# Strassen weight sums for gate and up: from VectorE subtractions to accumulating DMA transfers

## The chip, the core and the metric

The kernel runs on one core of a Trainium2 chip. Its engines work side by side, each with a queue of its own that it takes in order: TensorE (PE) multiplies matrices, VectorE (DVE) and ScalarE (ACT) do elementwise work, GpSimd (POOL) does little here, SyncE (SP) only issues DMA transfers. ACT and POOL can issue transfers as well. All of them run on the same 16 DMA engines. The metric is the device time of one execution in microseconds; lower is better.

## The reference

One decoder layer on 512 tokens of width 2048, in float32: a norm, four token mixers side by side, an output projection, and then the part that matters here, the feed-forward network:

```
def swiglu(h, w_gate, w_up, w_down):
    return (jax.nn.silu(h @ w_gate) * (h @ w_up)) @ w_down
...
        h = rmsnorm(x, norm_ffn_g[l])
        x = x + swiglu(h, w_gate[l], w_up[l], w_down[l])
```

`w_gate` and `w_up` are 2048 x 5632, `w_down` is 5632 x 2048.

## The kernel before

The stages follow one another: input projection and mixers, output projection (whose last pass also makes the sums of x for the next stage), gate and up, down, final norm.

*Exact products from rounded ones.* A float32 operand is split in two: ACT copies it into a rounded high half, DVE subtracts that from the operand to get the low half (`split2`, L1045; its two instructions carry the lines L1047 and L1048). Each product is three matmuls, high by high, high by low, low by high (L1297 to L1299).

*Strassen.* Gate and up are computed in 11 weight groups of 512 columns. In each group the tokens (two halves), the inputs (two halves, kh) and gate against up (f) form 2 x 2 blocks, and Strassen's scheme in Winograd's form takes seven block products in place of eight, in the order P1, P5, P6, P3, P7, P4, P2. P1, P3 and P2 take a weight block as it is, the other four take sums of weight blocks. A product is four steps of 12 matmuls (two input blocks of 128 rows, two token blocks, three matmuls each), so a group has 28 steps and the stage 308. Which sums of x a product takes is prepared once, in `first_sums` and `last_sums`, with their halves in `cmb`.

*Weights.* `w_dma` (L1113) issues the loads on SP, 256 KB each, into tiles wq, at most 12 at a time; blocks that two products need are loaded again (FRESH has five entries, so ten loads for each quarter of a group). `w_sum` (L1125) makes the sums on DVE: T = B12 - B11 for P5, B22 - T for P6, B21 - T for P4, in place in a tile T of 512 KB, and B22 - B12 for P7 (L1131, L1135, L1139, L1143). `w_split` (L1145) makes the two halves. High halves have 3 buffers, low halves 4.

*Order.* The program order is written out. Ahead of step k, `w_ahead` (L1157) makes sums for steps up to k+3 and splits for steps up to k+2, and issues loads for steps up to k+7:

```
        w_dma(k + 4)
        while sw["add"] < min(k + 4, len(steps)):
            ...
            w_sum(sw["add"])
            sw["add"] += 1
            if sw["split"] < min(k + 3, sw["add"]):
                w_split(sw["split"])
```

Results are read out of PSUM in `got_product` (L1253), by ACT (L1257, L1271) or by a DVE addition (L1266, L1268, L1275). `turn_h` (L1177) is side work spread over the following steps: it applies the norm and the gate, transposes h on PE, forms the sums of h for the down stage and stores them in DRAM from ACT's queue (hs, sh, sl, hT; ten stores of 256 KB a group). For the first group, the last sums of x (`late_sums`) run beside the first steps. POOL issues no transfer anywhere.

Of the kernel before, what the change touches and what calls it, by code (L numbers as in the profile page):

```python
# [8 lines left out]
F32 = mybir.dt.float32  # L9
F32R = mybir.dt.float32r  # L10
AF = mybir.ActivationFunctionType
OP = mybir.AluOpType
# [27 lines left out]
def hybrid_kernel(ctx, tc, xT, wi, wt, wo, wgu, wdn, vec, rows, sgw, w2a2, g2, pbias, cmask, oneh, addc, fing, out):  # L40
    nc = tc.nc
    pe, dv, ac, gp = nc.tensor, nc.vector, nc.scalar, nc.gpsimd
# [12 lines left out]
    def t2(name, shape=(128, 512), dt=F32):  # L55
        return p2.tile(list(shape), dt, name=name, tag="s2")
# [130 lines left out]
    for j in range(KT):  # L187
        t = t2("xraw")
# [829 lines left out]
    fp = sums.enter_context(tc.tile_pool(name="fp", bufs=4, reuse_waits="tile"))  # L1018
# [5 lines left out]
    norm2 = RowNorm()  # L1024
# [20 lines left out]
    def split2(hi, src, lo):  # L1045

        ac.activation(hi, src, AF.Copy)  # L1047
        dv.tensor_sub(lo, src, hi.bitcast(F32))  # L1048
# [8 lines left out]
    def first_sums(j):  # L1057

        a, b = xg[j], xg[j + 8]
        s12 = s2[j] = t2("s12")  # L1060
        dv.tensor_add(s12[:, lo_t], a[:, hi_t], b[:, hi_t])
        dv.tensor_sub(s12[:, hi_t], s12[:, lo_t], a[:, lo_t])
        h12, l12 = t2("h12", dt=F32R), t2("l12", dt=F32R)
        split2(h12, s12, l12)
        cmb["P5", j] = h12[:, lo_t], l12[:, lo_t]
        cmb["P6", j] = h12[:, hi_t], l12[:, hi_t]

        dv.tensor_sub(s12[:, lo_t], b[:, lo_t], s12[:, hi_t])

    def last_sums(j):  # L1070

# [22 lines left out]
    def ffn_norm():  # L1094
        while len(sqs) > 1:
            add_squares()
            yield
        for _ in range(8):
            yield
        norm2.add(sqs.pop(0))  # L1100
        norm2.root()
        yield


    ORDER = ("P1", "P5", "P6", "P3", "P7", "P4", "P2")
    FRESH = dict(P1=(0, 0), P5=(0, 1), P6=(1, 1), P7=(0, 1), P4=(1, 0))
    NGR = NG // 4
    steps = [(gi, p, jj) for gi in range(NGR) for p in ORDER for jj in range(4)]
    sw = dict(dma=0, add=0, split=0)
    raw, T, src, cut = {}, {}, {}, {}  # L1110
    RAWS = 12

    def w_dma(limit):  # L1113
        while sw["dma"] < min(limit, len(steps)):
            gi, p, jj = steps[sw["dma"]]
            if p in FRESH:
                if len(raw) + 2 > RAWS:
                    return
                kh, f = FRESH[p]
                for j in (2 * jj, 2 * jj + 1):  # L1120
                    t = raw[kh, f, j] = t2("wq")
                    nc.sync.dma_start(t, wgu[gi, kh, f, j])
            sw["dma"] += 1

    def w_sum(k):  # L1125
        gi, p, jj = steps[k]
        js = (2 * jj, 2 * jj + 1)
        if p == "P5":
            T[jj] = fp.tile([128, 2, 512], F32, name="T")
            for u, j in enumerate(js):  # L1130
                dv.tensor_sub(T[jj][:, u], raw.pop((0, 1, j)), raw.pop((0, 0, j)))  # L1131
            src[k] = T[jj]
        elif p == "P6":
            for u, j in enumerate(js):
                dv.tensor_sub(T[jj][:, u], raw[1, 1, j], T[jj][:, u])  # L1135
            src[k] = T[jj]
        elif p == "P4":
            for u, j in enumerate(js):
                dv.tensor_sub(T[jj][:, u], raw[1, 0, j], T[jj][:, u])  # L1139
            src[k] = T.pop(jj)  # L1140
        elif p == "P7":
            for j in js:
                dv.tensor_sub(raw[1, 1, j], raw[1, 1, j], raw.pop((0, 1, j)))  # L1143

    def w_split(k):  # L1145
        gi, p, jj = steps[k]
        hi = wp.tile([128, 2, 512], F32R, name="wh", tag="wraw", bufs=3)
        lo = wp.tile([128, 2, 512], F32R, name="wl", tag="wsp", bufs=4)
        if p in ("P5", "P6", "P4"):
            split2(hi, src.pop(k), lo)  # L1150
        else:
            for u, j in enumerate((2 * jj, 2 * jj + 1)):
                q = {"P1": (0, 0), "P3": (1, 1), "P7": (1, 1), "P2": (1, 0)}[p] + (j,)
                split2(hi[:, u], raw.pop(q) if p in ("P7", "P2") else raw[q], lo[:, u])
        cut[k] = hi, lo

    def w_ahead(k):  # L1157

        w_dma(k + 4)
        while sw["add"] < min(k + 4, len(steps)):  # L1160
            if sw["add"] >= sw["dma"]:
                w_dma(sw["add"] + 1)
            w_sum(sw["add"])
            sw["add"] += 1
            if sw["split"] < min(k + 3, sw["add"]):
                w_split(sw["split"])
                sw["split"] += 1
        while sw["split"] < min(k + 3, len(steps)):
            w_split(sw["split"])
            sw["split"] += 1  # L1170
        w_dma(k + 8)

    part = {}
# [3 lines left out]
    def turn_h(gi, th, h, us):  # L1177

        def put(p, t, u=0):
            nc.scalar.dma_start(ad[PI[p] + u, gi], t.rearrange("p (b t) -> p b t", b=2))  # L1180

        def high(p, src):
            hi = t2("sh", dt=F32R)
            ac.activation(hi, src, AF.Copy)
            put(p, hi.bitcast(F32))
            return hi

        def low(src, hi):
# [12 lines left out]
        if th == 0:  # L1201
            yield
            for t in range(2):
                ac.activation(h[t], h[t], AF.Silu, scale=rn[t])
        yield
        for t in range(2):
            dv.scalar_tensor_tensor(h[t], us[t], rn[t], h[t], op0=OP.mult, op1=OP.mult)
        us.clear()
        yield
        yield  # L1210
        p = turned(0)
        a = t2("hT")
# [36 lines left out]
        lo = low(p, hi)  # L1249
        yield  # L1250
        put("P2", lo.bitcast(F32), 1)
# [57 lines left out]
    for g in range(8):  # L1309
        def on_last(b, acc, g=g):  # L1310
            make_x2(g + 8 * b, acc)
            if b:
                split_a11(g)
                if g:
                    first_sums(g - 1)
                square_x2(g)
                square_x2(g + 8)
                if g:
                    add_squares()
                if g == 4:  # L1320
                    w_dma(4)
                if g == 6:
                    for j in range(3):
                        last_sums(j)
            elif g == 7:
                for j in range(3, 5):
                    last_sums(j)

        def early(g=g):
            if st["split"] < len(chunks):  # L1330
                issue_split()
            else:
                w_split(sw["split"])
                sw["add"] = sw["split"] = sw["split"] + 1
        brs = (2, 0)[g < 5:]
        run(gemm(len(brs), lambda c, k: (yh[brs[c], k], yl[brs[c], k]), on_last, early))
    for br in (0, 2):
# [306 lines left out]
def _layout(inp):  # L1644
# [15 lines left out]
    wt = np.ascontiguousarray(w.reshape(8, 2, 128, 4, 512).transpose(3, 0, 2, 1, 4))  # L1660
    wo = f("w_out")[0].reshape(2048, 2, 8, 128).transpose(0, 2, 1, 3)
    wo = np.ascontiguousarray(wo.reshape(4, 4, 128, 8, 256).transpose(3, 0, 2, 1, 4))
    gu = np.stack([f("w_gate")[0].reshape(2, 8, 128, 11, 512), f("w_up")[0].reshape(2, 8, 128, 11, 512)])
    wgu = np.ascontiguousarray(gu.transpose(4, 1, 0, 2, 3, 5))
    wdn = f("w_down")[0].reshape(11, 2, 2, 128, 2, 1024).transpose(0, 2, 1, 4, 3, 5)
    wdn = np.ascontiguousarray(wdn).reshape(22, 2, 2, 128, 1024)
    fing = f("norm_final_g").reshape(2, 1024)
# [31 lines left out]
```

## Time and profile before

| | |
|---|---|
| median of 3 runs | 2318.23 us (2317.65 to 2318.55) |
| profiled execution | 2319.38 us, span 2317.6 us |
| PE busy | 2231.3 us, 96% |
| DVE busy | 1562.3 us, 67% |
| ACT busy | 1014.6 us, 44% |
| POOL busy | 2.3 us, 16 instructions |
| gate and up stage | about 932 to 1836 us of the span |

A line is the line of the kernel's source; a helper's line stands for all its callers. A name such as wl<-wq,wh gives the tile written and those read. Busy time of PE is modelled, since matmuls are pipelined: the pace shows in the distance between their starts. Idle time is put down to what released the engine.

### The profile page before, as it was taken

The numbers are of one execution on the slowest core, as the hardware profiler recorded it, in microseconds if no ns is written. First come the engines' busy times: TensorE is split into PE (matmuls) and PEld (weight loads), VectorE is DVE, ScalarE is ACT, GpSimd is POOL, SyncE is SP. The second block draws the span as 40 slices with busy tenths as digits, with TensorE's granted clock in tenths as the row PEclk, the third lists the DMA queues.
The fourth block names the chain that finished last, engine by engine and source line by source line (L and its number), as shares of the span: only waits on it lengthen the run. The fifth ranks groups of instructions, "written<-read, shape, count | busy, mean of one in ns | idle before, by whom it ended". The sixth has DMA issues, their size and how long they took to land.

```text
span 2317.6 us, 29310 instructions
## 1 busy us (share of the span) xinstructions
PE 2231.3 (96%) x11064; PEld 1787.2 (77%) x11064; DVE 1562.3 (67%) x2345; ACT 1014.6 (44%) x1552; POOL 2.3 (0%) x16
## 2 busy tenths in 40 slices
PE   8999999999999998799999999999999799999996
PEld 6788878877777776587778778777877678888884
DVE  6555456654444456887877877887787677777765
ACT  5522231234445444544544454455445344543334
POOL 0000000000000000000000000000000000000000
PEclk9999999999999999899999999999999999999998
DMA  5222323222223334344653555465355277438884
GB/s 187 82 92 82 104 67 94 71 91 76 79 73 118 100 114 142 113 167 146 196 170 118 176 164 167 146 200 168 118 173 195 93 286 249 162 118 271 290 302 154
DMA packets 164542, 342.79 MB, mean 148 GB/s; under 512 B 29296, under 2 KB 34928, under 8 KB 164400
## 3 DMA queue, kind: packets, MB, share of 16 engines
q1 hardware_dynamic: 135408, 291.30, 38.9%
q10 hardware_dynamic: 28992, 49.61, 6.1%
q8 instruction: 87, 1.43, 0.3%
q14 instruction: 55, 0.45, 0.1%
HBM read 302.79 MB, written 38.05 MB: 147 GB/s over the span
## 4 chain that ended last, share of the span: by engine, by line
PE 82%; DVE 9%; ACT 4%; DMA 2%; issue 2%; ACTq 0%; SPq 0%; DVEq 0%
PE prod L1298 10%; PE prod L1299 10%; PE prod L1297 10%; PE acc L145 7%; PE acc L147 7%; PE acc L146 7%; PE bk L1383 5%; PE bk L1384 5%; PE bk L1382 5%; PE acc L166 3%; PE acc L168 3%; PE acc L167 3%; DVE wl L1048 2%; DMA wq<-in_wgu_dram 1%; ACT wh L1047 1%
## 5 line engine op out<-in xcount | busy, mean ns | idle before, releaser
L1048 DVE TENSOR_TENSOR wl<-wq,wh 128x512 fp32r<-128x512 f32 x352 | 227.0, 686 | 138.6 <-ACT wh L1047 137.5
L1298 PE MATMUL prod<-wl,h 128*128 128x512 f32 x704 | 276.8, 393 | 17.4 <-DVE wl L1048 17.4
L1047 ACT ACTIVATE wh<-wq 128x512 fp32r<-128x512 f32 x352 | 202.5, 623 | 186.7 <-PE prod L1299 112.1
L1297 PE MATMUL prod<-wh,h 128*128 128x512 f32 x704 | 276.4, 393 | 0.0
L1299 PE MATMUL prod<-wh,l 128*128 128x512 f32 x704 | 274.2, 390 | 0.0
L1382 PE MATMUL bk<-dh,ah 128*128 128x512 f32 x608 | 239.7, 394 | 25.5 <-ACT dh L1047 25.5
L107 DVE TENSOR_TENSOR wlo<-wraw,whi 128x1024 fp32r<-128x1024 f32 x127 | 155.3, 1223 | 148.0 <-ACT whi L106 147.7
L1383 PE MATMUL bk<-dl,ah 128*128 128x512 f32 x608 | 239.7, 394 | 3.2 <-DVE dl L1048 3.2
L1384 PE MATMUL bk<-dh,al 128*128 128x512 f32 x608 | 238.4, 392 | 0.0
L106 ACT ACTIVATE whi<-wraw 128x1024 fp32r<-128x1024 f32 x127 | 133.9, 1054 | 196.9 <-PE acc L146 94.3
L145 PE MATMUL acc<-xhi,whi 128*128 128x512 f32 x512 | 209.3, 409 | 5.3 <-ACT whi L121 5.2
L1047 ACT ACTIVATE wh<-T 128x1024 fp32r<-128x1024 f32 x132 | 140.2, 1062 | 153.2 <-PE prod L1299 83.5
L147 PE MATMUL acc<-xhi,wlo 128*128 128x512 f32 x512 | 201.0, 393 | 1.1 <-DVE wlo L107 1.1
L146 PE MATMUL acc<-xlo,whi 128*128 128x512 f32 x512 | 201.0, 393 | 0.3 <-DVE xlo L239 0.3
L1048 DVE TENSOR_TENSOR wl<-T,wh 128x1024 fp32r<-128x1024 f32 x132 | 161.0, 1220 | 36.2 <-ACT wh L1047 35.4
L1298 PEld LDWEIGHTS prod<-wl,h 128*128 128x128 f32 x704 | 132.2, 188 | 53.0 <-DVE wl L1048 26.6
L1297 PEld LDWEIGHTS prod<-wh,h 128*128 128x128 f32 x704 | 132.2, 188 | 29.9 <-ACT wh L1047 3.1
L1382 PEld LDWEIGHTS bk<-dh,ah 128*128 128x128 f32 x608 | 115.4, 190 | 50.9 <-ACT dh L1047 27.1
L1299 PEld LDWEIGHTS prod<-wh,l 128*128 128x128 f32 x704 | 132.2, 188 | 27.1
L1047 ACT ACTIVATE dh<-T 128x1024 fp32r<-128x1024 f32 x66 | 70.0, 1060 | 171.8 <-DVE T L1461 55.6
L1297 PE MATMUL prod<-wh,hb 128*128 128x512 f32 x352 | 140.1, 398 | 4.8 <-DVE c L1268 4.8
L1383 PEld LDWEIGHTS bk<-dl,ah 128*128 128x128 f32 x608 | 115.3, 190 | 30.5 <-DVE dl L1048 6.8
(316 smaller groups left out, 4155.9 us busy)
## 6 DMA issues: line engine op xcount, KB each, us to landing
wq<-in_wgu_dram SPq DMA_DIRECT2D x440, 256.0 KB, 3.5
rw<-in_wdn_dram SPq DMA_DIRECT2D x134, 512.0 KB, 4.9
wraw<-in_wi_dram SPq DMA_DIRECT2D x63, 512.0 KB, 3.6
wraw<-in_wt_dram SPq DMA_DIRECT2D x32, 512.0 KB, 3.6
wraw<-in_wo_dram SPq DMA_DIRECT2D x32, 512.0 KB, 3.7
ar<-ad SPq DMA_DIRECT2D x44, 256.0 KB, 3.9
ad<-sh ACTq DMA_DIRECT2D x33, 256.0 KB, 3.7
ad<-hs ACTq DMA_DIRECT2D x33, 256.0 KB, 4.1
```

Source lines behind the costliest of these rows:

```text
L107: dv.tensor_sub(lo, r, hi.bitcast(F32))
L145: pe.matmul(acc[b], wh, xh, start=(c == 0 and k == 0), stop=False)
L146: pe.matmul(acc[b], wh, xl, start=False, stop=False)
L147: pe.matmul(acc[b], wl, xh, start=False, stop=(c == nchunk - 1 and k == 3))
L1047: ac.activation(hi, src, AF.Copy)
L1048: dv.tensor_sub(lo, src, hi.bitcast(F32))
L1297: pe.matmul(acc[t], ah[:, tt], hi[:, u], start=first, stop=False, skip_group_check=more)
L1298: pe.matmul(acc[t], ah[:, tt], lo[:, u], start=False, stop=False, skip_group_check=more)
L1299: pe.matmul(acc[t], al[:, tt], hi[:, u], start=False, stop=(j == 7), skip_group_check=more)
L1382: pe.matmul(o, ah[:, a], hi[:, cc], start=fresh, stop=False, skip_group_check=True)
L1383: pe.matmul(o, ah[:, a], lo[:, cc], start=False, stop=False, skip_group_check=True)
L1384: pe.matmul(o, al[:, a], hi[:, cc], start=False, stop=last, skip_group_check=True)
```

## The change

The four kinds of weight sums are no longer made by DVE. The block is loaded into its tile, split for the product that takes it as it is, and then a DMA transfer issued from POOL adds the next block to the tile (accum_op=OP.add), after which the tile is split for the next product, and so on: tile X holds B11 for P1, B11 + B12 for P5, B11 + B12 + B22 for P6, and B11 + B12 + B22 + B21 for P4; tile wq holds B22 for P3 and B22 + B12 for P7. Since a transfer can only add, the signs of some sums of x are turned, and the up product comes out negated, which a negated norm factor (norm2.neg) takes back. Blocks for X come as one transfer of 512 KB, the layout of wgu is changed to suit; loads go from ten to six of 256 KB for each quarter of a group (two of them as one transfer), beside eight more of that size that add.

```diff
         s12 = s2[j] = t2("s12")
-        dv.tensor_add(s12[:, lo_t], a[:, hi_t], b[:, hi_t])
-        dv.tensor_sub(s12[:, hi_t], s12[:, lo_t], a[:, lo_t])
+        dv.tensor_sub(s12[:, lo_t], b[:, hi_t], a[:, hi_t])
+        dv.scalar_tensor_tensor(s12[:, hi_t], s12[:, lo_t], -1.0, a[:, lo_t], op0=OP.mult, op1=OP.subtract)
...
-        dv.tensor_sub(s12[:, lo_t], b[:, lo_t], s12[:, hi_t])
+        dv.scalar_tensor_tensor(s12[:, lo_t], s12[:, hi_t], -1.0, b[:, lo_t], op0=OP.mult, op1=OP.subtract)
...
-    FRESH = dict(P1=(0, 0), P5=(0, 1), P6=(1, 1), P7=(0, 1), P4=(1, 0))
+    LOADS = dict(P1=(0, 0), P3=(1, 1), P2=(1, 0))
+    ADDS = dict(P5=(0, 1), P6=(1, 1), P4=(1, 0), P7=(0, 1))
...
+            if p == "P1":
+                X[jj] = fp.tile([128, 2, 512], F32, name="T")
+                nc.sync.dma_start(X[jj].rearrange("p u n -> p (u n)"), wgu[gi, 0, 0, jj])
...
-    def w_sum(k):
...
+    def w_add(limit):
+
+        while sw["add"] < min(limit, len(steps)):
+            gi, p, jj = steps[sw["add"]]
+            if p in ADDS:
+                kh, f = ADDS[p]
+                if p == "P7":
+                    for u in range(2):
+                        gp.dma_start(raw["P3", 2 * jj + u], wgu[gi, kh, f, jj, :, u * 512:(u + 1) * 512], accum_op=OP.add)
+                else:
+                    gp.dma_start(X[jj].rearrange("p u n -> p (u n)"), wgu[gi, kh, f, jj], accum_op=OP.add)
+            sw["add"] += 1
...
+    def w_next():
+        w_dma(sw["split"] + 1)
+        w_add(sw["split"] + 1)
+        w_split(sw["split"])
+        sw["split"] += 1
+        w_add(sw["split"] + 4)
+
     def w_ahead(k):
 
-        w_dma(k + 4)
...
         while sw["split"] < min(k + 3, len(steps)):
-            w_split(sw["split"])
-            sw["split"] += 1
+            w_next()
         w_dma(k + 8)
...
-            dv.scalar_tensor_tensor(h[t], us[t], rn[t], h[t], op0=OP.mult, op1=OP.mult)
+            dv.scalar_tensor_tensor(h[t], us[t], norm2.neg[:, 2 * th + t:2 * th + t + 1], h[t], op0=OP.mult, op1=OP.mult)
```

## Rows read from the trace of the kernel before

**Rows 1.** Busy time by stage: us, PE, PEld, DVE, ACT, POOL, clock, DMA share, GB/s

```profile
932.00:1007.00 75.00, 65.80 (x262) 51.00 (x263) 67.38 (x106) 36.82 (x59) 0.00 (x0) 0.93 0.38 120
1007.00:1757.00 750.00, 734.54 (x3271) 597.68 (x3270) 589.81 (x856) 371.35 (x551) 0.00 (x0) 1.00 0.50 162
```

**Rows 2.** Groups by line, shapes apart: busy us, mean ns, idle before, releasers

```profile
L1298 PE MATMUL prod<-wl,h 128*128 128x512 f32 x704 | 276.8, 393 | 17.4 <-DVE wl L1048 17.4
...
L1297 PE MATMUL prod<-wh,hb 128*128 128x512 f32 x352 | 140.1, 398 | 4.8 <-DVE c L1268 4.8
```

**Rows 3.** The chain of waits over one group, in order of time

```profile
1165.08 0.61 DVE c L1268
...
1209.60 1.15 DVE wl L1048
1243.59 1.07 ACT wh L1047
1244.68 1.23 DVE wl L1048
1245.91 0.61 DVE c L1268
```

**Rows 4.** PE in order of time, in that group and in undisturbed steps

```profile
1165.82 0.47 PE L1297 MATMUL prod<-wh,hb 128*128 128x512 f32 x1 [0.43 <-DVE c L1268]
...
1207.26 0.50 PE L1298 MATMUL prod<-wl,h 128*128 128x512 f32 x1 [0.77 <-DVE wl L1048]
...
1210.79 0.50 PE L1298 MATMUL prod<-wl,h 128*128 128x512 f32 x1 [0.51 <-DVE wl L1048]
...
1232.46 0.39 PE L1297 MATMUL prod<-wh,h 128*128 128x512 f32 x1
...
1235.18 0.39 PE L1297 MATMUL prod<-wh,h 128*128 128x512 f32 x1
```

**Rows 5.** DVE and ACT in order of time, around the two late starts

```profile
1203.33 1.28 DVE L1131 TENSOR_TENSOR T<-wq 128x512 f32<-128x512 f32 x2
...
1203.44 0.34 ACTq L1180 DMA_DIRECT2D ad<-sl  x1
...
1208.21 1.06 ACT L1047 ACTIVATE wh<-T 128x1024 fp32r<-128x1024 f32 x1 [2.26 <-DVE hs L1246]
```

**Rows 6.** Groups by line, shapes apart: DVE instructions removed or changed

```profile
L1131 DVE TENSOR_TENSOR T<-wq 128x512 f32<-128x512 f32 x88 | 56.6, 683 | 0.0
...
L1207 DVE SCALAR_TENSOR_TENSOR c<-c,rn,c 128x512 f32<-128x512 f32 x44 | 31.1, 748 | 1.2 <-ACT c L1204 1.2
```

**Rows 7.** PE and DVE in order of time, in the first group

```profile
948.58 0.50 PE L1298 MATMUL prod<-wl,a 128*128 128x512 f32 x1 [2.11 <-DVE wl L1048]
...
954.45 0.50 PE L1298 MATMUL prod<-wl,h 128*128 128x512 f32 x1 [1.26 <-DVE wl L1048]
...
959.78 0.50 PE L1298 MATMUL prod<-wl,h 128*128 128x512 f32 x1 [2.21 <-DVE wl L1048]
...
963.92 0.50 PE L1298 MATMUL prod<-wl,h 128*128 128x512 f32 x1 [1.13 <-DVE wl L1048]
...
946.64 1.29 DVE L1131 TENSOR_TENSOR T<-wq 128x512 f32<-128x512 f32 x2
947.84 1.29 DVE L1048 TENSOR_TENSOR wl<-wq,wh 128x512 fp32r<-128x512 f32 x2
```

**Rows 8.** DMA queues and issues of 1007 to 1757 us; two issues of other stages

```profile
q1 hardware_dynamic: 52992, 96.49, 40.7%
q10 hardware_dynamic: 13212, 24.08, 8.5%
...
wq<-in_wgu_dram SPq DMA_DIRECT2D x369, 256.0 KB, 3.5
...
wraw<-in_wi_dram SPq DMA_DIRECT2D x63, 512.0 KB, 3.6
...
gain<-in_fing_dram ACTq DMA_DIRECT2D x2, 512.0 KB, 8.1
```

More of the change, by code (lines that the diff above doesn't have):

```diff
@@ L1101, in ffn_norm @@
         norm2.root()
+        norm2.neg = t1("rneg", (128, 4))
+        dv.tensor_scalar(norm2.neg, norm2.r, -1.0, None, op0=OP.mult)
         yield
     ORDER = ("P1", "P5", "P6", "P3", "P7", "P4", "P2")
-    FRESH = dict(P1=(0, 0), P5=(0, 1), P6=(1, 1), P7=(0, 1), P4=(1, 0))
+    LOADS = dict(P1=(0, 0), P3=(1, 1), P2=(1, 0))
+    ADDS = dict(P5=(0, 1), P6=(1, 1), P4=(1, 0), P7=(0, 1))
     NGR = NG // 4
@@ L1109, in hybrid_kernel @@
     sw = dict(dma=0, add=0, split=0)
-    raw, T, src, cut = {}, {}, {}, {}
+    raw, X, cut = {}, {}, {}
     RAWS = 12
@@ L1115, in w_dma @@
             gi, p, jj = steps[sw["dma"]]
-            if p in FRESH:
+            if p == "P1":
+                X[jj] = fp.tile([128, 2, 512], F32, name="T")
+                nc.sync.dma_start(X[jj].rearrange("p u n -> p (u n)"), wgu[gi, 0, 0, jj])
+            elif p in LOADS:
                 if len(raw) + 2 > RAWS:
                     return
[L1119 to L1122, printed above, removed]
+                kh, f = LOADS[p]
+                for u in range(2):
+                    t = raw[p, 2 * jj + u] = t2("wq")
+                    nc.sync.dma_start(t, wgu[gi, kh, f, jj, :, u * 512:(u + 1) * 512])
             sw["dma"] += 1
-    def w_sum(k):
[L1126 to L1143, printed above, removed]
+    def w_add(limit):
[4 more added lines that the diff above has]
+                if p == "P7":
+                    for u in range(2):
+                        gp.dma_start(raw["P3", 2 * jj + u], wgu[gi, kh, f, jj, :, u * 512:(u + 1) * 512], accum_op=OP.add)
+                else:
+                    gp.dma_start(X[jj].rearrange("p u n -> p (u n)"), wgu[gi, kh, f, jj], accum_op=OP.add)
+            sw["add"] += 1
     def w_split(k):
@@ L1148, in w_split @@
         lo = wp.tile([128, 2, 512], F32R, name="wl", tag="wsp", bufs=4)
-        if p in ("P5", "P6", "P4"):
-            split2(hi, src.pop(k), lo)
+        if p in ("P1", "P5", "P6", "P4"):
+            split2(hi, X.pop(jj) if p == "P4" else X[jj], lo)
         else:
             for u, j in enumerate((2 * jj, 2 * jj + 1)):
-                q = {"P1": (0, 0), "P3": (1, 1), "P7": (1, 1), "P2": (1, 0)}[p] + (j,)
-                split2(hi[:, u], raw.pop(q) if p in ("P7", "P2") else raw[q], lo[:, u])
+                split2(hi[:, u], raw["P3", j] if p == "P3" else raw.pop(("P3" if p == "P7" else p, j)), lo[:, u])
         cut[k] = hi, lo
-    def w_ahead(k):
-        w_dma(k + 4)
[L1160 to L1165, printed above, removed]
-                w_split(sw["split"])
-                sw["split"] += 1
+    def w_next():
[4 more added lines that the diff above has]
+        w_add(sw["split"] + 4)
+    def w_ahead(k):
         while sw["split"] < min(k + 3, len(steps)):
-            w_split(sw["split"])
-            sw["split"] += 1
+            w_next()
         w_dma(k + 8)
@@ L1332, in early @@
             else:
-                w_split(sw["split"])
-                sw["add"] = sw["split"] = sw["split"] + 1
+                w_next()
         brs = (2, 0)[g < 5:]
@@ L1662, in _layout @@
     wo = np.ascontiguousarray(wo.reshape(4, 4, 128, 8, 256).transpose(3, 0, 2, 1, 4))
-    gu = np.stack([f("w_gate")[0].reshape(2, 8, 128, 11, 512), f("w_up")[0].reshape(2, 8, 128, 11, 512)])
-    wgu = np.ascontiguousarray(gu.transpose(4, 1, 0, 2, 3, 5))
+    gu = np.stack([f(n)[0].reshape(2, 4, 2, 128, 11, 512) for n in ("w_gate", "w_up")])
+    wgu = np.ascontiguousarray(gu.transpose(5, 1, 0, 2, 4, 3, 6)).reshape(11, 2, 2, 4, 128, 1024)
     wdn = f("w_down")[0].reshape(11, 2, 2, 128, 2, 1024).transpose(0, 2, 1, 4, 3, 5)
```

## The prediction

> **What bounds the kernel now.** I read first the busy time by stage [rows 1]. The gate and up stage runs from 932 us to 1836 us, and from 1007 us on it is periodic: TensorE (PE) is busy 734.5 of 750 us at the full clock, VectorE (DVE) 590 us, ScalarE (ACT) 371 us. So 15.5 us of idle PE is all that anything but fewer matmuls can win in that stretch. The first 75 us are another case: PE is busy 65.8 us, at a mean granted clock of 0.93 (so a part of it at the lower of the two levels, 1.2 GHz), while DVE is busy 67.4 us. Nothing here bounds the stage by transfers: the DMA engines are busy 50%.
>
> Second, the groups by line, for what PE waits for [rows 2]. Of the idle time ahead of its matmuls, 17.4 us end with the low half of a split weight (wl, DVE), 4.8 us with a partial result read out by DVE (L1268). Third, the chain in order of time [rows 3] and PE's own order [rows 4]. A weight group lasts 80.83 us (the read-out at 1165.08 us comes again at 1245.91 us), and in each there are three places at which PE starts late. Two are in P5 and P6: the matmul at 1207.26 us starts 1.26 us after the one before it (0.77 us of it idle), that at 1210.79 us 0.90 us (0.51 us idle), where the pace is 2.72 us (1232.46 to 1235.18 us) / 12 = 0.23 us. They lose 1.03 + 0.67 = 1.70 us. The third, 0.82 us ahead of P4, is the read-out itself: 0.61 us on DVE beside three matmuls of PE.
>
> Fourth, DVE around the two places [rows 5]. Sums of weight blocks (L1131, 1.28 us a pair) stand on DVE's queue between what the side work needs (sl, hs, and so the next ACT instructions and the next wl). The late wl of [rows 3] (1209.60 us) stands in 10 of the 11 groups.
>
> **The change, part by part.**
>
> *Removed: 352 sums on DVE.* Four lines of 88 each, 56.6 us of busy time a line [rows 6]: 226 us, or 20.5 us of DVE in each of 11 groups. Nearly all of that lies beside matmuls, since PE is 98% busy. What stands on the path is the 1.70 us. Without the sums sl, hs and wl move up by the pair ahead of them, 1.2 us, against losses of 1.03 and 0.67 us, so both go: 10 x 1.70 = 17.0 us. Next late is then the add that feeds the split (below). The 0.82 us before P4 stays: no sum stands between, and the read-out starts as its matmuls end.
>
> *The first group.* DVE works without a pause and a pair of sums stands directly ahead of wl (946.64 us, then 947.84 us) [rows 7]. PE's four waits for wl are 2.11, 1.26, 2.21 and 1.13 us. Each loses the 1.2 us of its pair, the last one 1.1 us: 4.7 us. The 1.78 us wait for P1's second block comes from the sums of x and stays. That the clock of this stretch rises earlier I count at nothing; it could give some us more.
>
> *Added: 12 adding transfers of 512 KB and 8 of 256 KB a group, on the queue of GpSimd (POOL).* They bring 16 x 512 KB. No row shows an adding transfer, or any transfer from POOL. The row nearest in size is a plain 512 KB load, 3.6 us to landing [rows 8]. What a transfer holds the 16 engines for: 40.7% of 750 us over 369 loads of 256 KB is 0.83 us each, 1.65 us for 512 KB, which leaves 3.6 - 1.65 = 1.95 us around it. A store of h parts: 8.5% of 750 us over 92 is 0.69 us [rows 8]. So the bounds for 512 KB of sums are 1.65 us (a plain load; less can't be, since the same bytes come from HBM) and 6.15 us (the slowest 512 KB in the trace, 8.1 us to landing, less 1.95 us). I take 2.2 us: nearest the plain load, with a third more for reading the destination too.
>
> *Where they lie.* The split of step k starts when product k-2 starts, and takes 1.07 us on ACT and, to the end of DVE's part, 2.33 us [rows 3]. The add that follows waits for this split (it overwrites what was split) and must land before the split of step k+4. From the one to the other are 4 x 2.72 - 2.33 = 8.55 us before ACT waits, and 6 x 2.72 - 2 x 2.33 = 11.66 us before PE does. A single add needs 1.95 + 2.2 = 4.2 us. The eight adds of P5 and P6 come one behind another, and must all land in 13 x 2.72 - 2 x 2.33 = 30.7 us (33.4 us up to P3). In this time lie 7 stores of h parts (4.8 us) and P3's loads (4 x 1.65 = 6.6 us), so 8 x 2.2 + 4.8 + 6.6 + 1.95 = 31.0 us: it just fits. The adds of P7 and P4 have P2's loads beside them: 8 x 2.2 + 6.6 + 1.95 = 26.2 of 30.7 us. A whole group: 16 x 2.2 + 12 x 1.65 + 10 x 0.69 = 61.9 of 80.83 us. At a plain price it is 53.1 us, at 6.15 us 125 us.
>
> What an add that comes late holds up: ACT is in order, so behind the waiting wh stand the read-outs of products (L1257, L1271), the halves and copies of h (L1184, L1213) and the stores that ACT issues; PE waits for the first through its banks. On POOL the adds of later steps are queued behind the first; nothing else is there.
>
> The Trainium skill speaks against the price I take. Its page Collectives: The Full Stack (Part 3, on why ReduceScatter is half of AllGather) says that an add in a transfer costs its two source reads, so that it halves the rate. No run here shows this yet. By it the sum would be that of the first rival below.
>
> *Moved or small.* SP issues 20 transfers a group in place of 40, off the path; the loads for P1 become one of 512 KB, so its splits are one of 1.06 + 1.22 us in place of two halves, beside matmuls. Loads are issued up to eight steps ahead, as before. The sums of x get another form with a scalar, 748 ns against 683 ns for 512 elements [rows 6], some 0.03 us on 16 half-size ones in the first stretch, and one small negation: under 1 us, in a time when DVE has just lost 1.2 us per step. If no cover were left there, it would cost that 1 us.
>
> *Sum.* The profiled execution took 2319.38 us, of which the span is 2317.6 us. 2319.38 - 17.0 - 4.7 = 2297.7 us. The median of the runs lies 1.15 us below the profiled one, so I expect 2296.5 us, put at 2297: 0.9% faster.
>
> **Rivals.**
>
> *Each added byte costs the engines twice.* Place: the eight adds of P5 and P6, with P3's loads beside them. For it: an add must read its destination as well as its source. Against it: the second read is not from HBM, and the engines are idle half the time. Price: 3.3 us for 512 KB. The first run of adds then needs 26.4 + 13.35 = 39.8 us, against some 32 us (between 30.7 and 33.4): 7.8 us late; the second 26.4 + 8.55 = 35.0 us: 4.3 us late. 12.1 us x 11 - 21.7 = 111 us, so 2429 us. It decides from about 2.6 us on, where the first run is 2.0 us late per group and the whole gain is gone; between there and 3.3 us the time goes from 2318 to 2429 us.
>
> *More than twice.* Adding, or building descriptors on POOL (20 a group, two of 256 KB in each step of P7), runs well below the rate of plain loads. Nothing in the profile speaks for or against it, since POOL does 16 small instructions in all. Halfway from 3.3 to 6.15 us, at 4.7 us, a group needs 16 x 4.7 + 26.7 = 102 us of the engines, 21 us more than it lasts: 2318 + 11 x 21 = 2549 us; at the upper bound 125 us, 2800 us.
>
> *The waits stay.* The two late starts could be due to ACT's order alone: wh stands behind a store whose issue waits for sl, and behind an idle time of 2.26 us that ends with hs [rows 5]. For it: no sum is named there. Against it: on DVE, in order too, sl and hs have pairs of sums ahead of them. Then only the first group gains: 2313 to 2318 us.
>
> **How the numbers follow.** What a measurement of this kernel can tell from no change is 0.2%, that is 2313.6 to 2322.9 us. Adds that land in time, or cost less than they win: 0.53, with 2286 to 2313 us as their own range (the low end if the clock and the wait for P4 give 10 us more). Cancelled, because an add costs some 2.6 us (0.08) or because the waits stay (0.05): 0.13. Twice the price, from 2323 to 2430 us: 0.20. More than that: 0.14. So faster 0.53, same 0.13, slower 0.34. The range runs from 2286 to 2400 us: it leaves out the dearer third of the twice case (0.06) and all of the last (0.14).
>
> **What would show it.** Right: DVE in the periodic stretch near 43 us per 80 us, no idle of PE that ends with wl in P5 and P6, a period of about 79.1 us, adding transfers that land within 8.5 us, and a DMA share near 75%. Wrong: ACT's wh or PE's prod waiting for a transfer into T, a period above 81 us, a DMA share above 95% in P5 and P6, or landing times that grow from the first add of a run to its last. The second rival would show it in all steps, the first most in P6. If the wl waits stand where they stood with the adds long landed, it is the third.

## The result, and the profile after

The changed kernel takes 2347.5 us (median of four, 2343.2 to 2348.4) against 2318.4 us before (2317.7 to 2318.6): a ratio of 1.0123, 95% interval 1.0105 to 1.0140, so 1.2% slower where I forecast 0.9% faster. The profiled execution, the fastest of the four, took 2343.19 us, its span 2341.5 us, which is 23.8 us more than the profiled one before.

Where they went is read from the start of the first matmul of P4 in group 1 and in group 11, ten groups apart. Before, these are at 1003.90 and 1812.48 us, after at 999.17 and 1835.90 us:

```profile
1003.90 0.47 PE L1297 MATMUL prod<-wh,hb 128*128 128x512 f32 x1 [0.44 <-DVE c L1268]
...
1812.48 0.47 PE L1297 MATMUL prod<-wh,hb 128*128 128x512 f32 x1 [0.43 <-DVE c L1268]
```

```profile
999.17 0.47 PE L1294 MATMUL prod<-wh,hb 128*128 128x512 f32 x1 [0.39 <-DVE c L1265]
...
1835.90 0.47 PE L1294 MATMUL prod<-wh,hb 128*128 128x512 f32 x1 [2.73 <-DVE c L1265]
```

The first group is 4.73 us earlier; ten groups take 836.7 us in place of 808.6, 28.15 us more (83.67 us a group in place of 80.86); what follows takes 0.5 us more. -4.7 + 28.15 + 0.5 = +23.9 us. So the loss lies wholly in the periodic stretch.

The busy time in the periodic stretch of the changed kernel answers to [rows 1] (stretch, us, then PE, PEld, DVE, ACT, POOL, the granted clock, the DMA share, GB/s):

```profile
1007.00:1757.00 750.00, 718.79 (x3158) 577.96 (x3157) 408.27 (x511) 355.82 (x494) 156.93 (x180) 1.00 0.85 208
```

DVE has lost its sums, 590 to 408 us, as forecast. But PE has lost 15.7 us of busy time in these 750 us, the DMA engines are busy 85% in place of 50%, and the clock is 1.00 in the mean, as it was. By groups of 83.67 us PE idles 3.5 us in each, where it idled 1.7 us in 80.86 us; the other 1.0 us a group is in matmuls recorded longer (a first one after a pause shows 0.50 us, one in an undisturbed step 0.39 us).

A part of that 1.0 us is the clock after all. In groups 5, 8 and 11 it fell to the lower of the two levels, 1.2 GHz, right after PE's wait ahead of P4 (1.80, 2.35 and 2.73 us), and seven or eight matmuls follow one another at 0.43 us in place of 0.23 us. This is the slice of group 5:

```profile
1334.00:1338.00 4.00, 4.00 (x12) 3.19 (x11) 1.36 (x2) 0.13 (x1) 0.00 (x0) 0.59 0.91 328
```

That costs some 1.5 us each time, two of the three times within these 750 us, so about 0.3 us a group; the waits of 2.96 and 2.40 us in groups 2 and 4 left the clock where it was. In the kernel before it does not fall in this stretch. The three executions without a profile took 2347.1 to 2348.4 us at a mean clock of 0.984 to 0.985, where the profiled one shows 0.987. That their 4 to 5 us come from more such falls fits these figures, but no trace of them shows it.

The groups by line, over the whole run, answer to [rows 2]; the last is the issue of the 512 KB adds on POOL:

```profile
L1295 PE MATMUL prod<-wl,h 128*128 128x512 f32 x704 | 278.3, 395 | 15.2 <-DVE wl L1048 14.6
...
L1047 ACT ACTIVATE wh<-T 128x1024 fp32r<-128x1024 f32 x176 | 185.9, 1059 | 236.4 <-DMA T<-in_wgu_dram 117.9 <-PE prod L1296 58.5 <-DVE hs L1243 20.9
...
L1294 PE MATMUL prod<-wh,hb 128*128 128x512 f32 x352 | 142.1, 404 | 18.7 <-DVE c L1265 18.7
...
L1143 POOL DMA_DIRECT2D T<-in_wgu_dram x132 | 118.1, 917 | 1140.9 <-DVE x L1036 588.5 <-DVE wl L1048 524.1 <-DMA wq<-in_wgu_dram 20.6
```

The wait for wl that was to vanish is 14.6 us where it was 17.4 us. The wait for the read-out ahead of P4 has grown from 4.8 to 18.7 us. And ACT's wh, which feeds the splits, waits 117.9 us for transfers into T.

The DMA queues and issues of 1007 to 1757 us answer to [rows 8] (q0 is POOL's, q1 SP's; packets, MB, and the time of their packets as a share of 16 engines; then issues, KB each, median us to landing):

```profile
q0 software_dynamic: 25920, 75.51, 54.0%
q1 hardware_dynamic: 25822, 56.25, 21.6%
...
T<-in_wgu_dram POOLq DMA_DIRECT2D x108, 512.0 KB, 9.7
wq<-in_wgu_dram SPq DMA_DIRECT2D x144, 256.0 KB, 5.7
wq<-in_wgu_dram POOLq DMA_DIRECT2D x72, 256.0 KB, 9.1
T<-in_wgu_dram SPq DMA_DIRECT2D x35, 512.0 KB, 5.1
...
ad<-hs ACTq DMA_DIRECT2D x27, 256.0 KB, 11.5
```

The price of an add follows from them: 54.0% of 750 us is 405 us, over 108 adds of 512 KB and 72 of 256 KB (144 of the larger size): 2.81 us of the engines for 512 KB, where I took 2.2 us and put the turning point at 2.6 us. The plain loads still cost what they did: 21.6% of 750 us over 107 times 512 KB is 1.51 us. Everybody lands later: SP's loads in 5.7 us in place of 3.5, the stores of hs in 11.5 us in place of 4.1.

A share of 85% hides the shape. The same view in slices of 4 us, inside one group:

```profile
1176.00:1180.00 4.00, 4.00 (x19) 3.30 (x19) 2.00 (x4) 2.68 (x5) 0.00 (x0) 1.00 0.03 8
...
1188.00:1192.00 4.00, 4.00 (x20) 3.27 (x19) 2.92 (x4) 1.68 (x2) 0.87 (x1) 1.00 0.94 196
...
1200.00:1204.00 4.00, 4.00 (x22) 3.28 (x21) 2.26 (x3) 2.53 (x4) 0.82 (x2) 1.00 1.09 251
1204.00:1208.00 4.00, 3.51 (x16) 2.58 (x14) 1.24 (x2) 1.66 (x2) 0.43 (x1) 1.00 1.01 250
```

The engines stand still at 1176 to 1180 us (3%) and are full from 1188 us on. A share above 1.00 (1.09) means that the times of packets overlap. Over the whole group there would be room for the work, but it comes in blocks of adds. The chain of waits over this stretch, in order of time, shows how a full block passes its lateness on, and answers to [rows 3]:

```profile
1208.62 12.06 DMA ad<-hs
1220.75 0.33 SPq L1130
1221.17 2.83 DMA wq<-in_wgu_dram
1224.06 3.53 POOL wq L1141 x4
...
1232.38 12.20 DMA T<-in_wgu_dram
1244.69 1.07 ACT wh L1047
```

The store of hs takes 12.06 us, while the engines are full of P5's and P6's adds (4.1 us in the median before). SP waits for it (P3's load goes into a buffer that the store reads). P7's adds go into what this load brings, so POOL waits for it. P4's adds stand behind P7's on POOL, and the first is issued at 1232.38 us and lands 12.20 us later; only then can ACT split. PE in order of time, against [rows 4], shows the price:

```profile
1166.65 0.47 PE L1294 MATMUL prod<-wh,hb 128*128 128x512 f32 x1 [1.60 <-DVE c L1265]
...
1208.04 0.50 PE L1295 MATMUL prod<-wl,h 128*128 128x512 f32 x1 [0.53 <-DVE wl L1048]
...
1211.42 0.50 PE L1295 MATMUL prod<-wl,h 128*128 128x512 f32 x1 [0.33 <-DVE wl L1048]
...
1250.21 0.47 PE L1294 MATMUL prod<-wh,hb 128*128 128x512 f32 x1 [2.40 <-DVE c L1265]
```

At P4 the releaser named is a read-out of PE's own product (c, 0.6 us). It is late because it stands on DVE behind a wl, which waits for ACT's wh, which waits for the add:

```profile
1164.68 1.22 DVE L1048 TENSOR_TENSOR wl<-T,wh 128x1024 fp32r<-128x1024 f32 x1 [1.28 <-ACT wh L1047]
1165.83 1.28 DVE L1265 TENSOR_TENSOR c<-prod,c 128x512 f32<-128x512 f32 x2
```

The two late starts in P5 and P6 are there at almost the same places with no sum left on DVE (0.53 and 0.33 us idle, 0.77 and 0.51 us in [rows 4]). So two questions were open: what the late starts in P5 and P6 come from, and what in the adding transfers costs the time.

### The profile page after: what moved, and what is told of

The parts are those of the page before. It is cut to its first block, busy times and chain, and to the rows that moved or that the text cites. A ratio compares the mean times of both kernels' runs of the same rounds, so it can differ in the third digit from the quotient of the medians.

```text
span 2341.5 us, 29080 instructions
## 1 busy us (share of the span) xinstructions
PE 2240.9 (96%) x11064; PEld 1788.6 (76%) x11064; DVE 1357.1 (58%) x1950; ACT 1010.6 (43%) x1508; POOL 194.3 (8%) x236
## 4 chain that ended last, share of the span: by engine, by line
PE 56%; issue 17%; DMA 12%; DVE 7%; ACT 4%; POOL 3%; ACTq 0%; SPq 0%; POOLq 0%; DVEq 0%
DMA T<-in_wgu_dram 8%; PE acc L145 7%; PE acc L147 7%; PE acc L146 7%; PE bk L1379 5%; PE bk L1380 5%; PE bk L1378 5%; PE acc L166 3%; PE acc L168 2%; PE acc L167 2%; DMA wq<-in_wgu_dram 2%; POOL wq L1141 2%; PE prod L1294 2%; PE prod L1295 2%; PE prod L1296 2%
## 5 line engine op out<-in xcount | busy, mean ns | idle before, releaser
L1048 DVE TENSOR_TENSOR wl<-T,wh 128x1024 fp32r<-128x1024 f32 x176 | 214.8, 1224 | 267.8 <-ACT wh L1047 265.5
L1295 PE MATMUL prod<-wl,h 128*128 128x512 f32 x704 | 278.3, 395 | 15.2 <-DVE wl L1048 14.6
L1047 ACT ACTIVATE wh<-T 128x1024 fp32r<-128x1024 f32 x176 | 185.9, 1059 | 236.4 <-DMA T<-in_wgu_dram 117.9
L1048 DVE TENSOR_TENSOR wl<-wq,wh 128x512 fp32r<-128x512 f32 x264 | 173.1, 689 | 135.4 <-ACT wh L1047 134.5
L1047 ACT ACTIVATE wh<-wq 128x512 fp32r<-128x512 f32 x264 | 155.2, 625 | 134.7 <-PE prod L1296 75.2
L1143 POOL DMA_DIRECT2D T<-in_wgu_dram x132 | 118.1, 917 | 1140.9 <-DVE x L1036 588.5
L1294 PE MATMUL prod<-wh,hb 128*128 128x512 f32 x352 | 142.1, 404 | 18.7 <-DVE c L1265 18.7
```

What stands on the lines that cost most here:

```text
L1294: pe.matmul(acc[t], ah[:, tt], hi[:, u], start=first, stop=False, skip_group_check=more)
L1295: pe.matmul(acc[t], ah[:, tt], lo[:, u], start=False, stop=False, skip_group_check=more)
```

## The experiments

Each kernel was timed beside the kernel before on the same chip (2318.4 to 2319.5 us); ratios are to that. "Late c" is the wait ahead of P4.

**1. Is it the adding, or the transfers, or their issue on POOL?** The adds became plain loads of the same bytes by the same queue, so the sums are missing (the edit of the other transfer, for P7, is alike):

```
- gp.dma_start(..., wgu[gi, kh, f, jj], accum_op=OP.add)
+ gp.dma_start(..., wgu[gi, kh, f, jj])
```

> The transfers from POOL are plain loads into the same tiles at the same places (the additions are left out, so the weight sums are missing). Theory 1, an adding transfer holds the DMA engines longer than a plain load (2.81 us for 512 KB by the share of the POOL queue, against 1.65 us): the price falls to 1.6 to 1.8 us, landing from 9.7 us to 5 us or less, and the time to 2293 to 2305 us. Theory 2, the price is bearable and the order hurts (P3's loads wait on SP for buffers whose stores are not done, P4's adds stand behind P7's on POOL): the order is the same, so most of the loss stays, 2325 to 2345 us. Theory 3, a transfer issued by POOL is slow whatever it does: no change, 2343 to 2348 us.

And no such transfers at all (`if p in ADDS:` became `if p in ():`):

> No transfer is issued from POOL at all (the additions are left out). What is left is the gain from taking the sums off DVE with nothing put in their place. By the sum of the prediction 17.0 + 4.7 us: 2297 us. If the late wl in P5 and P6 are ACT's order and not the sums, 2313 us. All theories on the loss agree on this run; what it has less than the changed kernel is the price of the adds.

2308.6 us (0.9956, 0.9941 to 0.9971) and 2307.1 us (0.9952, 0.9935 to 0.9969). The first is some 4 us above what was expected if it is the adding (2293 to 2305 us) and far below what the other two theories gave; the second lies between the 2297 us of my sum and the 2313 us of ACT's order alone. So the same transfers as plain loads through POOL's queue cost 1.5 us, and making them add costs 38.9 us more. The queues of the plain kernel in 1007 to 1757 us, and POOL's line over the whole run:

```profile
q0 software_dynamic: 21856, 77.52, 32.5%
...
T<-in_wgu_dram POOLq DMA_DIRECT2D x113, 512.0 KB, 6.3
...
L1143 POOL DMA_DIRECT2D T<-in_wgu_dram x132 | 69.9, 532 | 1167.7 <-DVE x L1036 588.5 <-DVE wl L1048 569.1 <-DMA wq<-in_wgu_dram 7.1
```

32.5% of 750 us over 149 times 512 KB is 1.64 us: the adding makes it 2.81 us, 1.72 times. The Trainium skill (Collectives: The Full Stack, Part 3, on why ReduceScatter is half of AllGather) says of ReduceScatter that its add needs two source reads, which halves the rate; for the adding transfers of this kernel the trace agrees in direction, at 1.72 times the price and not 2.

The second kernel carries the other half. With the sums gone and nothing in their place, the time falls by 11.3 us only, where I had counted 21.7, and both late starts stay, though smaller: at 1119.96 and 1123.32 us PE starts 0.48 and 0.73 us after the matmul before, where it was 1.26 and 0.90 us. PE and, ahead of it, ACT in that kernel:

```profile
1123.32 0.50 PE L1295 MATMUL prod<-wl,h 128*128 128x512 f32 x1 [0.34 <-DVE wl L1048]
...
1120.54 0.36 ACTq L1177 DMA_DIRECT2D ad<-hs  x1
1120.94 1.06 ACT L1047 ACTIVATE wh<-T 128x1024 fp32r<-128x1024 f32 x1 [2.30 <-DVE hs L1243]
```

ACT waits 2.30 us for hs, as it waited 2.26 us in [rows 5]: not for its own operand, but because the issue of a store of hs stands ahead of wh on ACT. That was my third rival.

**2. Does it help to start P1's and P3's loads earlier?** If the loss is the chain from the store of hs over SP to P7 and P4, loads issued sixteen steps ahead should win most of it back.

```
...
- w_dma(k + 8)
+ w_dma(k + 16)
```

A guard beside it stops the loads for P1 while the tile of the group before is still to be split for P4.

> Plain loads are issued up to 16 steps ahead in place of 8, so that P3's loads can run in the 12 us of each group in which the DMA engines do nothing. Theory 1: the same bytes at the same price, but the eight adds of P5 and P6 no longer share the engines with 6.6 us of loads, 29 us in place of 36 us for a place of 31 to 33 us: DVE's read-out before P4 and the wl waits in P6 shrink, 2318 to 2328 us. Theory 2, P3's loads come late because of the buffers of stores, and P7's and P4's adds behind them: the same change takes most of the loss away, 2300 to 2318 us. Theory 3: 2343 to 2348 us, as adds are slow by themselves.

2327.4 us (1.0040, 1.0025 to 1.0055): 20 of the 40 us are back, and a group is 82.12 us. PE's groups by line over the whole run:

```profile
L1297 PE MATMUL prod<-wl,h 128*128 128x512 f32 x704 | 279.2, 397 | 19.3 <-DVE wl L1048 19.0
...
L1296 PE MATMUL prod<-wh,hb 128*128 128x512 f32 x352 | 140.2, 398 | 4.2 <-DVE c L1267 4.2
```

Late c is 4.2 us, where it was 18.7 us; the waits for wl do not go, 19.0 us against 14.6. The adds are as many as they were, and in the slices from 1188 to 1216 us the engines are as full (1.03 to 1.08). So I put the wait ahead of P4 down to the chain over the store and SP's loads. The run does not divide it cleanly from the load on the engines: the edit also takes P3's loads out of the block, and the time lies in the range that was expected from full engines (2318 to 2328 us), not in that of the chain alone (2300 to 2318 us).

**3. Is it only the order on POOL?** P4's adds issued ahead of P7's, as soon as P6 is split.

```
+ p = dict(P1="P5", P5="P6", P6="P4", P3="P7").get(p)
```

> The adds for P4 are issued directly behind the splits for P6 and so ahead of the adds for P7 on POOL. Theory 1: the engines are saturated there, the bytes only change places: the wait before P4 (18.7 us in all) goes and comes back in P3 or P7, 2338 to 2350 us. Theory 2: P4's adds were late only because of POOL's order: the wait before P4 falls from 18.7 us to about 5 us, and the time by some 14 us or more, 2325 to 2334 us. Theory 3: as theory 2, since a slow transfer that is issued 8 steps earlier is no longer late: 2325 to 2334 us.

2395.3 us (1.0342, 1.0318 to 1.0367): far worse, and outside what any of the theories gave. The wait ahead of P4, which all three had shrink, is 18.8 us over the run, where it was 18.7, and the waits for wl grow from 14.6 to 33.4 us. SP's and POOL's transfers of 256 KB then land in

```profile
wq<-in_wgu_dram SPq DMA_DIRECT2D x131, 256.0 KB, 13.0
...
wq<-in_wgu_dram POOLq DMA_DIRECT2D x64, 256.0 KB, 15.4
```

SP's loads, for P3 and P2, took 5.7 us and P7's adds 9.1 us in the changed kernel. By the order of issue twelve adds of 512 KB now follow one another in place of eight, and P3's loads meet them. That the order on POOL alone was the fault is refuted; that adds close together are what hurts is in line with this run, not shown by it.

**4. How many adds are too many?** With loads sixteen steps ahead, only a part of the sums is made by transfers, the others by DVE, from plain loads, as before. Edit, a part of the first (the others alike):

```
- ADDS = dict(P5=(0, 1), P6=(1, 1), P4=(1, 0), P7=(0, 1))
+ ADDS = dict(P5=(0, 1), P6=(1, 1))
...
```

P5 and P6, eight of 512 KB in a block:

> Half of the change: sums for P5 and P6 by adding transfers, those for P7 and P4 by DVE from plain loads; loads up to 16 steps ahead. Theory 1 (an add holds the DMA engines 2.8 us for 512 KB, 1.7 times a plain load, and the engines are saturated by 16 of them): a group then needs 8 x 2.81 + 16 x 1.64 + 10 x 0.69 = 56 us of the engines in place of 72 us, so adds land in time and nearly all of what the run without adds gained comes back: 2307 to 2314 us. Rival (it is the latency of each add that hurts, not the load on the engines): P5 and P6 keep their late starts of the run with 16 steps ahead, 2320 to 2328 us.

P7 and P4:

> The other half: sums for P7 and P4 by adding transfers, those for P5 and P6 by DVE; loads up to 16 steps ahead. Theory 1: the engines are not saturated, so no loss by adds, but the sums that stood ahead of wl in P5, P6 and in the first group are on DVE again, so no gain either: 2316 to 2322 us. Rival (latency): the wait before P4 comes back, 2325 us or more.

P5 alone, four:

> A quarter of the change: only P5's sums by adding transfers, the others by DVE; loads up to 16 steps ahead. Theory 1: a group needs 4 x 2.81 + 20 x 1.64 + 10 x 0.69 = 51 us of the engines; the first group keeps most of its gain (P5's sums stood ahead of wl there), P6 its late start: 2309 to 2316 us. Rival (latency): no better than the run with P5 and P6, 2315 to 2325 us.

2322.9 us (1.0020, 1.0010 to 1.0029), 2322.0 (1.0013, 1.0004 to 1.0022), 2313.3 (0.9973, 0.9964 to 0.9983). The first misses the 2307 to 2314 us that the standing theory gave and lies in the range of its rival, the latency of each add (2320 to 2328 us): half the adds still lose against before, though the share of 750 us has fallen to 68%. The other two came out about as theory 1 had them (2316 to 2322 and 2309 to 2316 us). Slices of that first kernel and the time that ACT's wh waits for transfers into T in 1007 to 1757 us (us, times, longest), then slices of P5 alone:

```profile
1200.00:1204.00 4.00, 3.45 (x16) 2.54 (x15) 2.43 (x3) 1.35 (x2) 0.86 (x1) 1.00 1.05 289
1204.00:1208.00 4.00, 3.64 (x16) 2.71 (x15) 2.45 (x2) 2.35 (x3) 0.86 (x1) 1.00 1.06 274
...
ACT wh L1047 <- DMA T<-in_wgu_dram: 56.5, 27, 3.6
```

```profile
1200.00:1204.00 4.00, 3.83 (x17) 2.84 (x16) 3.79 (x6) 1.31 (x3) 0.00 (x0) 1.00 0.53 163
1204.00:1208.00 4.00, 3.48 (x16) 2.56 (x15) 4.00 (x6) 2.68 (x4) 0.00 (x0) 1.00 0.63 212
```

Through a block of eight the engines stay full; behind a block of four they have room at the same place (0.53 and 0.63). What PE loses in these slices does not tell the two apart: it loses in both (3.45 and 3.64 against 3.83 and 3.48 of 4 us), at the old late starts of P5 and P6. What does is ACT's wait for transfers into T, 56.5 us with eight and none with four, and a late start in P3 that only the first kernel has (0.48 us idle at 1217.74 us). One add per step of 2.72 us takes 2.81 us, so by this price a block of eight with anything beside it can't keep up, whatever the rest of the group does. The rival is not refuted by these runs, since landing and load move together: adds land in 8.5 us in blocks of eight and in 6.6 us in blocks of four.

**5. Do the stores' issues on ACT make the late starts?** In the kernel before, with all its sums on DVE, only the queue that issues the ten stores of h parts a group changed:

```
- nc.scalar.dma_start(ad[PI[p] + u, gi], ...)
+ nc.gpsimd.dma_start(ad[PI[p] + u, gi], ...)
```

> The kernel before, with the ten stores of h parts in a group issued by POOL in place of ACT. The run without transfers still started late in P5 and P6, with ACT waiting for hs and sl. If that is because ACT, in order, issues the stores of hs and sl and so waits for DVE ahead of the next wh (the prediction's third rival), most of 1.70 us a group goes without any sum taken away: 2300 to 2308 us. If the sums on DVE are the cause, no change: 2315 to 2320 us.

2296.9 us (0.9905, 0.9888 to 0.9922): more than was expected (2300 to 2308 us), 21.4 us faster than the kernel before in the result above (22.6 us than the same kernel beside it) and 51 us faster than the changed one; it beats both. Ten groups take 788.5 us, 78.85 each. In its trace the store waits on POOL, which has nothing else to do, and ACT goes on; in 1007 to 1757 us PE waits for wl no more:

```profile
1195.45 1.04 ACT L1047 ACTIVATE wh<-T 128x1024 fp32r<-128x1024 f32 x1
1196.39 1.07 ACT L1257 ACTIVATE c<-prod 128x512 f32<-128x512 f32 x2
...
1197.82 1.07 ACT L1047 ACTIVATE wh<-T 128x1024 fp32r<-128x1024 f32 x1
...
1201.65 0.54 POOL L1180 DMA_DIRECT2D ad<-hs  x1 [1.87 <-DVE hs L1246]
...
L1298 PE MATMUL prod<-wl,h 128*128 128x512 f32 x589 | 229.1, 389 | 0.0
```

The Trainium skill (DMA: Bandwidth & Descriptors, "Issuing engines are not separate DMA queues") has it that issuing from several engines saves only the time that their sequencers take to start a transfer, usually small beside the transfer. The issue itself is 0.33 us on ACT here, which agrees; what counted is the wait ahead of it on an engine that works in order.

**6. Are sums on DVE worth anything once the stores are off ACT?** The kernel without transfers (experiment 1, second) with its stores on POOL:

> The changed kernel without any adding transfer (the additions are left out), and with the stores of h parts by POOL: what taking the sums off DVE is worth once ACT no longer waits to issue stores. If the sums cost nothing in the periodic stretch, only the first group gains against the stores alone: 2291 to 2294 us. If each pair of sums still stands on the path there, 2280 to 2288 us.

2286.7 us (0.9861, 0.9846 to 0.9876). By its time alone that is the other theory's range, each pair of sums still on the path (2280 to 2288 us); the trace says otherwise. A group takes 78.77 us against 78.85: all of DVE's sums taken off the periodic stretch win 0.08 us a group, which is nothing. Its lead of 10 us lies at the ends: 4.7 us in the first group, and a shorter pause of PE at the start of the down stage (6.45 against 10.53 us). The busy times of 1007 to 1757 us, with the sums on DVE and without them:

```profile
1007.00:1757.00 750.00, 746.01 (x3355) 614.09 (x3354) 606.18 (x883) 376.33 (x565) 53.93 (x100) 1.00 0.51 169
```

```profile
1007.00:1757.00 750.00, 746.47 (x3358) 614.63 (x3357) 433.31 (x543) 375.87 (x527) 53.94 (x100) 1.00 0.36 117
```

DVE is busy 173 us less and PE gains 0.5 us.

**7. Can adds and moved stores be joined?** All adds with loads sixteen ahead; P5's alone; and P5's and P6's in the first group only, where DVE works without a pause:

> The whole change with loads up to 16 steps ahead and the stores of h parts by POOL (behind the adds on its queue). If the price of the adds (2.8 us each for 512 KB) is what is left of the loss in the run with 16 steps ahead, the engines are still busy about 88% and P5 and P6 still wait: 2305 to 2322 us. If what was left there was ACT's order, 2291 to 2298 us. If stores that stand behind waiting adds come too late for the buffers of loads, 2325 us or more.

> P5's sums by adding transfers in all groups, the others on DVE, loads up to 16 steps ahead, stores of h parts by POOL. With four adds a group the engines are not full (51 of 79 us), so the first group's 4.7 us come on top of the stores: 2290 to 2295 us. If even four adds a group delay stores or splits, 2297 to 2305 us.

> Stores of h parts by POOL, and adding transfers for P5 and P6 in the first weight group alone; all other sums on DVE. If the sums on DVE cost time only where DVE is full (the first group), the 4.7 us that all runs with transfers or without sums won there add to what the stores won: 2290 to 2294 us against 2297 us with the stores alone. If the 4.7 us come back later (DVE or ACT behind in the first group anyway), 2296 to 2298 us.

2328.9 us (1.0041, 1.0026 to 1.0056), 2297.6 (0.9909, 0.9894 to 0.9924), 2298.1 (0.9910, 0.9893 to 0.9926). All adds lose 32 us against experiment 5, in the range expected if stores behind waiting adds come too late for the buffers of loads (2325 us or more): in 1007 to 1757 us SP waits 232.0 us for stores of hs, 105.5 us in the changed kernel. Some 12 us of it are the clock, which stands at the lower level for 23.9 of these 750 us (0.98 in the mean), after late starts in P3.

P5's alone neither win nor lose, and the last missed. In both P4 of group 1 is earlier than in experiment 5, by 4.7 and 4.2 us, and ten groups take as long (788.4 us), but PE's pause at the start of the down stage is 15.62 and 17.45 us in place of 10.53 us, so the gain is gone. The traces show a part of the way: ACT waits there 9.86 and 11.69 us ahead of a half (ah) of a stored part of h (ar), whose load SP issues at 1824.12 and 1824.54 us; in experiment 5 the first load of that line goes out at 1811.52 us and ACT does not wait for it. With P5's adds SP stands until 1823.25 us, when a store of sh has landed that POOL issued at 1819.43 us. Why SP comes to this wait in the one kernel and not in the other I did not find. That it is the landing of POOL's last stores was tried, with the stores of the last group back on ACT:

> The kernel before with stores of h parts by POOL, but those of the last weight group by ACT as before. If stores by POOL land later and so hold up the begin of the down stage, the idle PE there (10.5 us) gets shorter and the time 2290 to 2295 us. If that idle time is set by the work on h and the loads that follow, 2296 to 2299 us.

2298.5 us (0.9910, 0.9895 to 0.9926), a pause of 12.28 us, not shorter, with that load at 1829.73 us behind a store of sh from ACT. That stays open.

**8. Is it the bytes of the adds, or their number?** Half the bytes in as many transfers (`[:, :512]` in both operands), and half as many transfers of full size (`if p in ADDS and jj % 2 == 0:`):

> The changed kernel with every adding transfer at half its size (the other half of the additions is left out): as many adds, in the same places, half the bytes. If the bytes in a run of adds are what counts, the adds of a step need 1.4 us of 2.72 us and land in time: 2307 to 2314 us, near the run without transfers. If each add has a fixed cost on the path, 2330 to 2347 us.

> The changed kernel with adding transfers for every other step only (the others are left out): half as many adds of full size, the same bytes as with half-size adds. Bytes count: 2307 to 2316 us, like half-size adds. A fixed cost for each add: half of the loss stays, 2322 to 2330 us, well below the time with half-size adds.

2308.3 us (0.9951, 0.9935 to 0.9967) and 2310.2 (0.9958, 0.9943 to 0.9973). Either halving takes away nearly the whole loss (2307.1 us is the time without any transfer). As the first leaves the number of adds and of their issues as it was, it isn't these that cost the time; and as half the bytes cost at most some 3 us and all of them 40, the loss isn't in proportion to the bytes. It goes with ACT's wait for transfers into T in 1007 to 1757 us, in the changed kernel, with half size and with half the number:

```profile
ACT wh L1047 <- DMA T<-in_wgu_dram: 103.6, 52, 4.1
...
ACT wh L1047 <- DMA T<-in_wgu_dram: 21.4, 14, 3.1
...
ACT wh L1047 <- DMA T<-in_wgu_dram: 22.4, 9, 4.3
```

That the loss sets in where the engines can't keep up with a block of adds is in line with this. A full slice alone does not make it: within a group slices of 4 us reach 1.07 and 1.04 in these two kernels as well. Their queues in 1007 to 1757 us, first half size, then half the number:

```profile
q0 software_dynamic: 26507, 38.83, 33.4%
```

```profile
q0 software_dynamic: 13248, 38.80, 31.2%
```

33.4% and 31.2% of 750 us over 74 times 512 KB are 3.4 and 3.2 us for 512 KB, more than 2.81 us, though the engines are busy only 66% and 64% of the 750 us. The price isn't a constant; why it is higher with fewer bytes the runs don't tell.

## Why the prediction failed, step by step

*Sums removed, 17.0 us in ten groups: wrong, and the first step that failed.* I took the pairs of sums ahead of wl on DVE as the cause of the two late starts. Experiment 5 removes both starts with every sum in place and wins 20.1 us in ten groups; the second kernel of experiment 1 removes every sum and wins 7.1 us (80.86 to 80.15 us a group), and experiment 6 wins 0.7 us by it once the stores are off ACT. The cause was ACT's order: the issue of a store waits for sl or hs and the next wh waits behind it. The row was there, ACT's 2.26 us for hs in [rows 5], and I gave it 0.05. My argument against it, that DVE's order delays sl and hs too, holds for a third of the gain and no more.

*The first group, 4.7 us: right as a sum.* 4.73 us, and 5.3 us without the transfers. It did not come wait by wait: PE's idle time up to P4, its first wait left out, falls from 9.2 to 4.9 us, but the wait of 1.78 us that was to stay is 0.57 us, one of 0.90 us for wh is new, and the first matmul starts 0.5 us later. That the sum agrees to a tenth is luck.

*An add at 2.2 us: the step that set the sign.* It takes 2.81 us, above the point of 2.6 us from which I had the first rival decide. By that rival's own formula the first block takes 8 x 2.81 + 13.35 = 35.8 us against some 32 us, 3.8 us late, and the second 22.5 + 8.55 = 31.0 us against 30.7, 0.3 us late: 4.1 x 11 - 21.7 = 23 us, so 2319.4 + 23 = 2343 us, where the profiled execution took 2343.19 us. That agreement is partly luck. The formula gives the adds 45 us and the gain 21.7; the runs show 40.4 us (against no transfers) and 11.3 us, and the median execution took 2347.5 us.

*The place: half right.* I put the first rival in P5 and P6. The block there is where the engines are full, but most of what PE idles more than before shows ahead of P4 (18.7 us, which I had as 0.82 us a group that "stays"). What I left out is the way between them: a late store of hs holds SP, which holds P3's loads, which hold P7's adds, which hold P4's on POOL. I had named the queue on POOL and not the buffers that SP waits for. With the loads of experiment 2 that wait is 4.2 us.

*Budget over the run, "it just fits", 31.0 of 30.7 to 33.4 us:* the right sum to make, and one that left no margin for a price taken from a plain load. At 2.81 us it is 35.8.

*What would show it:* DVE came out at 44 us per 80 us (forecast 43), the DMA share at 85% (75), the period at 83.67 us (79.1), the landing at 9.7 us (8.5 at most). The signs named for the first rival are all there: ACT's wh waits for T, the period is above 81 us, the share above 95% within the blocks, and the landing times grow, from 5.8 us for the first of the eight adds issued from 1187 us on to 9.1 us for the last. Those of the third are there too, wl late in its old places with the adds gone. Both rivals were right at once in what they named, the first at 2.81 us and not its 3.3, and each accounts for its part: the loss by the first, the missing gain by the third. Even adds for nothing would have given 2307 us and not 2297.

*More than twice:* ruled out, at 1.72 times. POOL takes 0.92 us to issue an add (0.53 us a plain load), and as many issues of plain loads cost 1.5 us in all.

## What to carry to other kernels

Price an adding transfer at 1.7 times a plain one of the same bytes or more (2.8 to 3.4 us here against 1.64), and make the budget over the block in which the adds come one after another, not over a period: here engines that were 50% free in the mean before were full where the block stood. Where a wait is named after a compute instruction, look at what stands ahead of it on its engine: an issue of a store that waits for its data blocks an in-order engine, and moving ten such issues a group to an idle engine won 20 us in ten groups, where taking 20 us a group of work off DVE then won under 1 us in the same stretch. Before relieving an engine, check that it is late by its own work.

## What the runs showed of the hardware

- By the times of its packets an adding transfer into SBUF held the 16 engines 2.81 us for 512 KB, a plain one by the same queue 1.64 us; with adds of half the size, or half as many, it was 3.4 and 3.2 us for 512 KB.
- Plain loads by POOL's queue held the engines no longer than SP's did in the kernel before, 1.64 us for 512 KB against 1.65 us. In the kernel with plain loads 512 KB landed later by POOL than by SP, in 6.3 us against 3.6 us, and 256 KB earlier, in 3.6 us against 5.4 us.
- Beside the blocks of adds the transfers of other queues landed later: ACT's stores of sh, sl and hs, 256 KB each, in 8.7 to 11.5 us, in the kernel before in 3.5 to 4.1 us.
- The issue of an add kept POOL 0.92 us in the mean (most of them 0.86 us), that of a plain load 0.53 us.
- The granted clock of TensorE fell to 1.2 GHz after some waits of 1.80 to 2.73 us in a stretch that was otherwise busy, and not after others of 2.40 and 2.96 us; each fall cost some 1.5 us.
